# Hybrid encoder block on one core: wide column sums and a new order in the opening, v stores on ScalarE's queue, and two fourth weight sums on GpSimd

## The chip, the cores and the metric

The kernel runs on one core of a Trainium2 chip, in one launch. The time is the device time in microseconds (us) of that core. The engines are TensorE (PE in the profile; its weight loads are shown as PEld), VectorE (DVE), ScalarE (ACT), GpSimd (POOL) and SyncE (SP), which here only issues DMAs. TensorE's products go to PSUM; the other operands lie in SBUF.

## The reference

One encoder layer in float32 on 1024 positions of width 1024, then a final RMSNorm. Cut to what matters here:

```python
ada = silu(c) @ w_ada + b_ada                 # 6 x 1024 values: shift1, scale1, gate1, shift2, scale2, gate2
h = rmsnorm(x, g_mix) * (1 + scale1) + shift1
qa, ka, va, qb, kb, vb, ga, gb = split(h @ w_in)
oa = mixture_of_dilations(qa, ka, va, rel_bias)
ob = neighbourhood_attention_2d(qb, kb, vb, na_rpb)
x = x + gate1 * ((sigmoid(ga) * (oa @ w_branch_dil) + sigmoid(gb) * (ob @ w_branch_na)) @ w_out)
h2 = rmsnorm(x, g_ffn) * (1 + scale2) + shift2
u_val, u_gate = split(conv3(h2 @ w_up))
x = x + gate2 * ((gelu(u_gate) * u_val) @ w_down)
y = rmsnorm(x, g_final)
```

## The kernel before

**Products in three parts.** Nearly every large product is made of three TensorE products of a reduced-precision type: an operand is split into a high half, made by a ScalarE copy, and a low half, the operand less that copy, made by VectorE or GpSimd (`split`, L57 and L61). The three are high x high, high weight x low, low weight x high. So every weight tile passes through ScalarE and VectorE or GpSimd ahead of its product, and so does every tile of h.

**The layout.** x and h are held transposed, as 8 tiles (k = 0 to 7) of 128 features by 512 positions, for two halves of the positions. The program is one function, written out in stages. In the opening (the `with tc.manual_schedule` block, L419 to L610) the order of every engine's instructions is the order of the code. Most of the attention and of the feed-forward part lies outside such blocks: there a scheduler, which simulates a timeline, sets the order, so it can shift far away from an edit.

**The opening.** Needed first is h = x * rstd * (1 + scale1) * g_mix + shift1, the names being `am1` for (1 + scale1) * g_mix and `ada` for the shifts. The first 2048 columns of w_ada are loaded in four pieces (`wt[0]` to `wt[3]`, 8 rows t of 128 x 512 each). Piece q gives shift and scale for the tile pair k = 2q, 2q + 1, so the loop `for q in range(4)` makes h pair by pair. A piece is summed over its 1024 rows in two ways together: `ada_rows` multiplies rows by a column of `cs` (silu of c) and adds them up on VectorE (L174, L176; the running sum `acc` lies in PSUM, the last one goes back into the row's own tile), and `ada_sums` (L160) brings the sum across partitions on TensorE, with each 128 x 128 block of a row as weights and one column, of `cs` or of ones, as the moving operand: four matmuls of one column, a "narrow four". A row that goes straight to `ada_sums` with its column of `cs` is spared VectorE. `piece_bias` (L293, L295) then writes `ada` and `am1`.

At the same time ScalarE squares the tiles of x, VectorE adds the squares, `add_sums` (L98) sums them across partitions, `rs` becomes the reciprocal root (L458, L459, L461), `bcast` (L111) spreads it over the partitions in PSUM (`pb`, with a copy `pbs` in SBUF by ScalarE, L470), and x is multiplied by it: tiles 0 to 3 on VectorE (L473, L481), 4 to 7 on GpSimd (L487). `scaled` makes the high half of h (L229, ScalarE), a full copy (L230, ScalarE) and, when called later, the low half (L231, VectorE). With them run `qk_products` (L310, first q and k tile) and `v_parts` (L320, first v columns).

Between the narrow fours stand `warm(n, ...)` matmuls (L236) of a matrix of ones, 128 columns each, whose result is dropped: they only keep TensorE running.

SyncE's queue issues the loads in the order of the code: x, the small vectors, w_ada piece 0, half of the first weights of q and k (`half_load`), half of v's, piece 1, the other halves, piece 2, piece 3, the second half of x. An issue there also waits for an earlier transfer to land.

**The v products.** `v_out` (L285) copies a v product from PSUM to a buffer `vs` (two of them) on ScalarE and stores it by SyncE's queue (L287). In the loop over `v_steps` these stores alternate in SyncE's queue with loads of later w_ada pieces (`pair_load`, L135), whose rows VectorE sums (`row_pairs`). The loop covers nine of twelve steps; the rest follows it.

**The first w_up tiles.** A w_up tile's product is done by seven products of half size (Strassen's scheme in Winograd's form). `a_operands` makes its weight operands from the quarters a11, a12, a21, a22: S1, S2 and S3 on GpSimd (L1255 to L1257), the fourth sum S4 = a12 - S2 on VectorE (L1273), each followed by a split. It is a generator; each `next` issues one more portion. Tiles t = 0, 1 and 2 are interleaved, with the operands of h2 made in between: each tile of x is multiplied by the broadcast rstd (`scale`, L1622), added or subtracted (L1625, L1631, L1645), and split (L1442, L1443, L1236, L1237).

```python
        pair(ws, ("S2", "S1"), *s_tiles())
        S4 = S1 if apart else a12
        if w_at != 3:
            dve.tensor_tensor(S4, a12, S2, OP.subtract)
        yield
        pair(raw[1], ("S3", "22"), *s_tiles())
```

Of the kernel before, what the change touches and what calls it, by code (L numbers as in the profile page):

```python
# [18 lines left out]
D = 1024  # L19
# [10 lines left out]
def hybrid_encoder(tc, xT, c, w_ada, small, w_in, p1_bias, p23_bias, na_bias, ln2_mult, ident, w_br, w_out,  # L30
# [62 lines left out]
    qkpool = tc.alloc_tile_pool(name="qk", bufs=4)  # L93

# [189 lines left out]
    def v_out(br, st, p, c0=0):  # L284
        vs = work.tile([128, 512], FT, name="vs", bufs=2)[:, :p.shape[-1]]  # L285
        act.activation(vs, p, AF.Copy)
        sp.dma_start((va_s, vb_c)[br][st * 128:st * 128 + 128, c0:c0 + p.shape[-1]], vs)  # L287
# [17 lines left out]
    def qk_products(ks):  # L305
        for k in ks:
            mhi, mlo = h[0, k]
            for x_, (part, m) in enumerate(((0, mhi), (1, mhi), (0, mlo))):
                for p, w in zip(qk_psum, qk_w):
                    pe.matmul(p, w[part][:, k], m, start=k + x_ == 0, stop=k == KT - 1 and x_ == 2)  # L310
# [108 lines left out]
    with tc.manual_schedule(engines={e.engine for e in (sp, act, dve, pool, pe)}):  # L419
# [26 lines left out]
        warm(35, idle, True)  # L446
# [6 lines left out]
        pcol = ps_n.tile([128, KT], FT, name="pcol")  # L453
# [4 lines left out]
        dve.tensor_scalar(r, pcol[:, :4], 1.0 / D, EPS, OP.mult, OP.add)  # L458
        act.activation(r, r, AF.Sqrt)  # L459
        ada_rows(wt[0], acc, range(3, 4), 3, 7)  # L460
# [15 lines left out]
        for q in range(4):  # L476
            ks = range(2 * q, 2 * q + 2)
            piece_bias(q, pa)
            if q == 0:
                for k in range(2, 4):  # L480
                    dve.tensor_tensor(x[0][k], x[0][k], pb, OP.mult)  # L481
                stage = [ps_n.tile([128, 512], FT, name=n) for n in ("pcol", "pbc")]
            low = [scaled(x[0][k], k) for k in ks]
            if q == 0:
                v_split(v_raw, (pool, pool), slice(0, 4), v_w[0])
                for k in range(4, 8):
                    pool.tensor_tensor(x[0][k], x[0][k], pbs, OP.mult)  # L487
# [18 lines left out]
            qk_products(ks)  # L506
            if q == 0:
                pa = ada_sums([(wt[1][t], cs[:, t:t + 1]) for t in (6, 7)], stop=False)
                v_parts(0, range(4), ks, (0,))
                ada_sums([(wt[1][5], ones)], pa)  # L510
                v_parts(0, range(4), ks, (1, 2))
                continue
            v_parts(0, (0,), ks, range(3))
# [26 lines left out]
        row_ends = (4, 7, 10, 12, 14, 17, 19, 22, 24)  # L540
# [37 lines left out]
        for n, step in enumerate(v_steps[:9]):  # L578
# [50 lines left out]
    for br, st in v_steps[9:]:  # L629
        v_out(br, st, *v_wide(st))  # L630
# [612 lines left out]
    def a_operands(raw, n, work, st, lo_eng=pool, last=False, w_at=0, spot=None, apart=False):  # L1243
# [5 lines left out]
        S2, S1 = ws[:, 0], ws[:, 1]  # L1249

# [18 lines left out]
        yield  # L1269
        pair(ws, ("S2", "S1"), *s_tiles())  # L1270
        S4 = S1 if apart else a12
        if w_at != 3:
            dve.tensor_tensor(S4, a12, S2, OP.subtract)  # L1273
        yield
        pair(raw[1], ("S3", "22"), *s_tiles())
# [313 lines left out]
    prep.append(a_operands(raw.pop(1), 4, s_home, sts[1], dve, spot=extra))  # L1589
# [94 lines left out]
    nxt = a_operands(raw.pop(2), 4, s_home, sts[2], w_at=None, spot=extra)  # L1684
# [225 lines left out]
```

## Time and profile before

| | |
|---|---|
| three timed runs, us | 1501.8, 1496.16, 1500.61; median 1500.61 |
| profiled execution, us | 1498.67 |
| its span, first to last instruction, us | 1496.8 |
| mean granted TensorE clock | 0.998 of full speed |
| DMA | 210.29 MB, mean 140 GB/s |

Times in the profile count from the span's start. A row of the timeline gives start, duration, engine, line, operation, the tiles out<-in with shapes, how many instructions it merges, and in brackets the idle time of the engine before it with the instruction that ended it. A float32 matmul leaves two records, so a narrow four shows as x8. Matmuls overlap, and a busy TensorE may still be one that streams fillers.

### The profile page before, as it was taken

What the parts mean: (1) busy time and instruction counts of PE and PEld (TensorE: products, weight loads), DVE (VectorE), ACT (ScalarE), POOL (GpSimd) and SP (SyncE); (2) the same over time, 40 slices, a digit from 0 to 9 for tenths busy, and PEclk for the clock granted to TensorE, in tenths of its full rate; (3) what the DMA queues carried; (4) which work ended last, traced back from release to release, by engine and by line L of the source; (5) the groups of instructions that cost most, each with busy time, mean ns of one, the idle gap of its engine ahead of it and who ended that gap; (6) DMA issues with size and microseconds to landing.
All of it is one profiled execution on the core that took longest, in us unless ns stands there. A gap on an engine that the chain in (4) does not pass through costs nothing.

```text
span 1496.8 us, 21659 instructions
## 1 busy us (share of the span) xinstructions
PE 1474.4 (98%) x7664; PEld 1251.9 (84%) x7664; DVE 939.0 (63%) x1763; ACT 773.6 (52%) x1442; POOL 760.6 (51%) x633
## 2 busy tenths in 40 slices
PE   9999999999999999999999999999999999999997
PEld 8888888889798998888888778888888888877887
DVE  7683446465555665556515897666666667886865
ACT  4531666666655666653345464444444447474542
POOL 3031332434234454512268668766666776978811
PEclk9999999999999999999999999999999999999999
DMA  9577332444645555577544313222222233542313
GB/s 371 183 277 268 88 99 68 143 114 129 170 144 145 144 160 166 172 243 260 194 153 143 104 43 141 85 85 85 85 83 84 71 136 116 197 148 64 104 41 113
DMA packets 117301, 210.29 MB, mean 140 GB/s; under 512 B 42788, under 2 KB 55716, under 8 KB 117156
## 3 DMA queue, kind: packets, MB, share of 16 engines
q1 hardware_dynamic: 116632, 208.57, 43.4%
q8 instruction: 60, 0.98, 0.3%
q14 instruction: 49, 0.40, 0.1%
q10 hardware_dynamic: 560, 0.33, 0.1%
HBM read 163.58 MB, written 42.66 MB: 138 GB/s over the span
## 4 chain that ended last, share of the span: by engine, by line
PE 81%; DVE 5%; POOL 5%; DMA 4%; issue 2%; ACT 2%; SPq 0%; DVEq 0%; POOLq 0%; ACTq 0%
PE pj L84 10%; PE pj L86 10%; PE pj L85 10%; PE pj L1308 10%; PE pj L1307 10%; PE pj L1306 10%; PE pj L402 3%; PE O L1013 2%; DMA wraw<-w_down 2%; PE T L1000 1%; PE S L978 1%; POOL wsl L61 1%; PE pv L279 1%; PE pv L281 1%; PE pv L280 1%
## 5 line engine op out<-in xcount | busy, mean ns | idle before, releaser
L61 POOL TENSOR_TENSOR wlo<-wraw,whi 128x512 fp32r<-128x512 f32 (+1 forms) x84 | 106.1, 1284 | 144.8 <-ACT whi L57 129.8
L84 PE MATMUL pj<-h,whi 128*128 128x512 f32 x432 | 178.1, 412 | 0.4 <-DVE kl L374 0.4
L86 PE MATMUL pj<-h,wlo 128*128 128x512 f32 x432 | 169.8, 393 | 0.0
L85 PE MATMUL pj<-h,whi 128*128 128x512 f32 x432 | 169.4, 392 | 0.0
L1306 PE MATMUL pj<-op,wsh 128*128 128x512 f32 x408 | 159.1, 391 | 3.7 <-ACT wsh L57 2.7
L1307 PE MATMUL pj<-op,wsh 128*128 128x512 f32 x408 | 159.1, 390 | 0.9 <-DVE op L1237 0.6
L1308 PE MATMUL pj<-op,wsl 128*128 128x512 f32 x408 | 157.8, 390 | 0.7 <-POOL wsl L61 0.7
L667 DVE TENSOR_TENSOR tl<-T,th 128x512 fp32r<-128x512 f32 (+3 forms) x120 | 77.2, 654 | 101.2 <-ACT th L666 99.9
L717 POOL TENSOR_TENSOR wlo<-wraw,whi 128x512 fp32r<-128x512 f32 x58 | 74.4, 1293 | 126.8 <-ACT whi L716 126.7
L61 POOL TENSOR_TENSOR wsl<-big,wsh 128x512 fp32r<-128x512 f32 (+1 forms) x86 | 111.7, 1320 | 42.5 <-ACT wsh L57 37.6
L659 ACT ACTIVATE P<-P,st 128x256 f32<-128x256 f32 x128 | 64.2, 503 | 93.9 <-DVE st L658 93.9
L1543 DVE SCALAR_TENSOR_TENSOR big<-pj,sm,big 128x512 f32<-128x512 f32 (+2 forms) x183 | 94.9, 563 | 16.5 <-ACT big L1537 15.6
L86 PEld LDWEIGHTS pj<-h,wlo 128*128 128x128 f32 x432 | 81.1, 188 | 18.0
L1306 PEld LDWEIGHTS pj<-op,wsh 128*128 128x128 f32 x408 | 76.6, 188 | 21.9 <-ACT wsh L57 4.0
L1307 PEld LDWEIGHTS pj<-op,wsh 128*128 128x128 f32 x408 | 76.6, 188 | 18.2 <-DVE op L1237 1.2
L1308 PEld LDWEIGHTS pj<-op,wsl 128*128 128x128 f32 x408 | 76.6, 188 | 17.4 <-POOL wsl L61 1.8
L84 PEld LDWEIGHTS pj<-h,whi 128*128 128x128 f32 x432 | 81.5, 189 | 11.5 <-issue 0.8
L1308 PE MATMUL pj<-op,wlo 128*128 128x512 f32 x232 | 90.3, 389 | 0.0
L1307 PE MATMUL pj<-op,whi 128*128 128x512 f32 x232 | 90.3, 389 | 0.0
L1306 PE MATMUL pj<-op,whi 128*128 128x512 f32 x232 | 90.3, 390 | 0.0
L85 PEld LDWEIGHTS pj<-h,whi 128*128 128x128 f32 x432 | 81.7, 189 | 10.1
L61 POOL TENSOR_TENSOR wsl<-wraw,wsh 128x384 fp32r<-128x384 f32 (+1 forms) x46 | 57.3, 1268 | 62.1 <-ACT wsh L57 54.5
(398 smaller groups left out, 4173.6 us busy)
## 6 DMA issues: line engine op xcount, KB each, us to landing
wraw<-w_in SPq DMA_DIRECT2D x32, 512.0 KB
wada<-w_ada SPq DMA_DIRECT2D x31, 512.0 KB
big<-w_up SPq DMA_DIRECT2D x22, 512.0 KB
wraw<-w_up SPq DMA_DIRECT2D x22, 512.0 KB
big<-as SPq DMA_DIRECT2D x22, 512.0 KB
as<-big SPq DMA_DIRECT2D x21, 512.0 KB
gs<-gs SPq DMA_DIRECT2D x32, 256.0 KB
g<-gs SPq DMA_DIRECT2D x16, 512.0 KB
```

What stands on the lines that cost most here:

```text
L61: lo_eng.tensor_tensor(lo[:, i:i + step], raw[:, i:i + step], f(hi)[:, i:i + step], OP.subtract)
L84: pe.matmul(psum, whi[:, k0 + k], mhi, start=k == 0, stop=False)
L85: pe.matmul(psum, whi[:, k0 + k], mlo, start=False, stop=False)
L86: pe.matmul(psum, wlo[:, k0 + k], mhi, start=False, stop=k == n - 1)
L402: pe.matmul(p[:, 256 * r:256 * r + 256], ww[:, k], m[:, r], start=k + x + r == 0, stop=k == KT - 1 and x == 2, skip_group_check=True)
L659: act.activation(pp, pp, AF.Exp, bias=mi, scale=-1.0, accum_out=li)
L667: dve.tensor_tensor(tl[:m, :n], pt[:m, :n], f(th)[:m, :n], OP.subtract)
L717: pool.tensor_tensor(lo[:, i:i + n], raw[:, i:i + n], f(hi)[:, i:i + n], OP.subtract)
L1306: pe.matmul(psum, whi[:, k], bhi, start=j < 4 and k == 0, stop=False, skip_group_check=True)
L1307: pe.matmul(psum, whi[:, k], blo, start=False, stop=False, skip_group_check=True)
L1308: pe.matmul(psum, wlo[:, k], bhi, start=False, stop=k == n - 1, skip_group_check=True)
L1543: dve.scalar_tensor_tensor(y[:, dst], src, wt, y[:, dst], OP.mult, OP.add)
```

## The change

1. **Wide sums.** `wide_sums` does the sum of a row of blocks with the column spread over 128 columns: four matmuls of 128 columns instead of one, every column of a block holding the same sum; `every` reads the first column of each block. It is used for the square sums and for pieces 0 and 1 of w_ada. The fillers between them go; in front stand 38 instead of 35, before the first product 4 instead of 5.
2. **Opening order.** The first VectorE row of piece 0 stands ahead of the rstd instructions and one more ahead of the reciprocal. The second pair's multiplies move from VectorE to GpSimd. Row 3 of piece 1 goes to TensorE alone. For pieces 2 and 3, two rows instead of two and three stand ahead of the next `piece_bias`.
3. **Load order.** Piece 1 stands ahead of v's first halves, and piece 2 ahead of the second halves of q, k and v.
4. **v stores.** In the loop over `v_steps` the stores go to ScalarE's queue, and the loop has one step more.
5. **Fourth sums.** `a_operands` takes `s4_at`; for tile 1 (3) and tile 2 (2) S4 is a GpSimd instruction at that portion.

```diff
+    def wide_sums(dst, blocks, col, first=False):
+        for m in range(4):
+            cc = slice(m * 128, m * 128 + 128)
+            pe.matmul(dst[:, cc], blocks[:, cc], col.to_broadcast([128, 128]), start=first and m == 0, stop=False,
+                      skip_group_check=True)
+    def every(p):
+        return p.rearrange("p (t c) -> p t c", c=128)[:, :, 0]
...
+        wt.append(ada_load(1))
         half_load(v_raw, (8, 9), 0)
-        wt.append(ada_load(1))
+        wt.append(ada_load(2))
         half_load(qk_raw, (0, 4), 1)
         half_load(v_raw, (8, 9), 1)
-        wt.append(ada_load(2))
         wt.append(ada_rows_load(3))
...
-        warm(35, idle, True)
+        warm(38, idle, True)
...
-        add_sums(pcol, total, True, True)
-        warm(3, idle, True)
-        pa = ada_sums([(wt[0][0], cs[:, 0:1])], stop=False)
+        wide_sums(pcol, total, ones, True)
+        pa = ps_s.tile([128, 512], FT, name="pada", bufs=1)
+        for t in range(2):
+            wide_sums(pa, wt[0][t], cs[:, t:t + 1], t == 0)
         r = wpool.tile([128, KT], FT, name="rs", bufs=2)[:, :4]
-        dve.tensor_scalar(r, pcol[:, :4], 1.0 / D, EPS, OP.mult, OP.add)
+        ada_rows(wt[0], acc, range(3, 4), 3, 7)
+        dve.tensor_scalar(r, every(pcol), 1.0 / D, EPS, OP.mult, OP.add)
         act.activation(r, r, AF.Sqrt)
-        ada_rows(wt[0], acc, range(3, 4), 3, 7)
+        ada_rows(wt[0], acc, range(4, 5), 3, 7)
         dve.reciprocal(r, r)
         qk_split(0, (pool, pool))
         pb = bcast(r, ps_n, "pbc")
-        warm(3, idle, True)
-        ada_sums([(wt[0][1], cs[:, 1:2])], pa, stop=False)
-        warm(4, idle, True)
-        ada_sums([(wt[0][2], cs[:, 2:3])], pa, stop=False)
-        warm(2, idle, True)
+        wide_sums(pa, wt[0][2], cs[:, 2:3])
...
-        ada_rows(wt[0], acc, range(4, 8), 3, 7)
+        ada_rows(wt[0], acc, range(5, 8), 3, 7)
...
-        ada_sums([(wt[0][7], ones)], pa)
-        warm(5, idle, True)
+        wide_sums(pa, wt[0][7], ones)
+        warm(4, idle, True)
...
             if q == 0:
-                for k in range(2, 4):
-                    dve.tensor_tensor(x[0][k], x[0][k], pb, OP.mult)
...
-                for k in range(4, 8):
+                for k in range(2, 8):
                     pool.tensor_tensor(x[0][k], x[0][k], pbs, OP.mult)
...
-            steps = (range(q + 1, 4), range(4, 5), range(5, 7)) if q else (range(0), range(2), range(2, 6))
+            steps = (range(2, 4), range(4, 5), range(5, 7)) if q else ((), (0,), (1, 2, 4, 5))
...
-                ada_rows(wt[q + 2], acc, range(q + 2), 0, 6)
+                ada_rows(wt[q + 2], acc, range(2), 0, 6)
...
+                qk_products((0,), range(2))
+                pa = ps_s.tile([128, 512], FT, name="pada", bufs=1)
+                wide_sums(pa, wt[1][3], cs[:, 3:4], True)
+                qk_products((0,), range(2, 3))
+                qk_products((1,))
...
-                    v_out(step[0], st, pp)
+                    v_out(step[0], st, pp, queue=act)
...
+        if s4_at == 2:
+            pool.tensor_tensor(S4, a12, S2, OP.subtract)
         pair(ws, ("S2", "S1"), *s_tiles())
-        if w_at != 3:
+        if w_at != 3 and not s4_at:
             dve.tensor_tensor(S4, a12, S2, OP.subtract)
         yield
+        if s4_at == 3:
+            pool.tensor_tensor(S4, a12, S2, OP.subtract)
```

TensorE's line in the opening, from the square sums to the first product of h. Before (`pcol` holds the square sums, `pada` those of w_ada, `om` the fillers' ones, `kl` and `qs` the tiles of w_ada piece 0):

```order
L236 MATMUL pv<-om 128x128 x35
L98 MATMUL pcol<-ones,sq 128x1 x4
L236 MATMUL pv<-om 128x128 x3
L160 MATMUL pada<-cs,kl 128x1 x4
L111 MATMUL pbc<-idt,rs 128x128 x4
L236 MATMUL pv<-om 128x128 x4
L160 MATMUL pada<-cs,qs 128x1 x4
L236 MATMUL pv<-om 128x128 x2
L160 MATMUL pada<-ones,qs 128x1 x4
L236 MATMUL pv<-om 128x128 x5
L310 MATMUL pj<-h,whi 128x512 x2
```

And now:

```order
L246 MATMUL pv<-om 128x128 x38
L99 MATMUL pcol<-ones,sq 128x128 x4
L99 MATMUL pada<-cs,kl 128x128 x8
L121 MATMUL pbc<-idt,rs 128x128 x4
L99 MATMUL pada<-cs,qs 128x128 x4
L99 MATMUL pada<-ones,qs 128x128 x4
L246 MATMUL pv<-om 128x128 x4
L321 MATMUL pj<-h,whi 128x512 x2
L321 MATMUL pj<-h,wlo 128x512 x2
L99 MATMUL pada<-cs,wada 128x128 x4
L321 MATMUL pj<-h,whi 128x512 x4
```

The last sum of piece 0 (`pada<-ones,qs`) has no filler ahead of it any more but follows the third row's sum directly, and the sum of piece 1's row 3 has come between the first pair's products.

VectorE's line where the rstd of h2 for the second half of the positions is ready and the tiles of x are multiplied by it. Before (`wraw<-wraw,xb` is S4 of tile 1, `x<-x,pbc` with their numbers the multiplies):

```order
L103 TENSOR_SCALAR rs<-pcol 128x4
L105 RECIPROCAL rs<-rs 128x4
L1273 TENSOR_TENSOR wraw<-wraw,xb 128x512
L1622 TENSOR_TENSOR x_8240<-x_8240,pbc 128x512
L1622 TENSOR_TENSOR x_8277<-x_8277,pbc 128x512
```

GpSimd's line at the same place, now (`xb` and `wraw` hold the sums of tile 1, `wsl` their low halves):

```order
L1269 TENSOR_TENSOR xb<-wraw 128x512
L1270 TENSOR_TENSOR xb<-xb,wraw 128x512
L1271 TENSOR_TENSOR wraw<-wraw 128x512
L1291 TENSOR_TENSOR wraw<-wraw,xb 128x512
L61 TENSOR_TENSOR wsl<-xb,wsh 128x512 x2
L61 TENSOR_TENSOR xb<-wraw,xb 128x512
```

The S4 row has left VectorE's line, where the multiply now follows the reciprocal, and stands on GpSimd ahead of the low halves of S1 and S2. Behind w_up's first tiles the order of w_up and w_down is shifted in places on all engines, which no line of the diff says.

More of the change, by code (lines that the diff above doesn't have):

```diff
@@ L282, in v_wide, with v_out @@
         return ps
-    def v_out(br, st, p, c0=0):
+    def v_out(br, st, p, c0=0, queue=sp):
         vs = work.tile([128, 512], FT, name="vs", bufs=2)[:, :p.shape[-1]]
         act.activation(vs, p, AF.Copy)
-        sp.dma_start((va_s, vb_c)[br][st * 128:st * 128 + 128, c0:c0 + p.shape[-1]], vs)
+        queue.dma_start((va_s, vb_c)[br][st * 128:st * 128 + 128, c0:c0 + p.shape[-1]], vs)
     sig = wpool.tile([128, KT], FT, name="rs", bufs=2)
@@ L303, in qk_split, with qk_products @@
             split(raw[:, 4 * i:4 * i + 4], hi[:, 4 * i:4 * i + 4], lo[:, 4 * i:4 * i + 4], e)
-    def qk_products(ks):
+    def qk_products(ks, parts=range(3)):
         for k in ks:
             mhi, mlo = h[0, k]
-            for x_, (part, m) in enumerate(((0, mhi), (1, mhi), (0, mlo))):
+            for x_ in parts:
+                part, m = ((0, mhi), (1, mhi), (0, mlo))[x_]
                 for p, w in zip(qk_psum, qk_w):
@@ L577, in hybrid_encoder @@
         due = {}
-        for n, step in enumerate(v_steps[:9]):
+        for n, step in enumerate(v_steps[:10]):
             if step is None:
@@ L628, in hybrid_encoder @@
     first_w = w_split(ahead.pop(1), pool)
-    for br, st in v_steps[9:]:
+    for br, st in v_steps[10:]:
         v_out(br, st, *v_wide(st))
@@ L1241, in hybrid_encoder, with a_operands @@
     names = tuple(b for _, b in STEPS)
-    def a_operands(raw, n, work, st, lo_eng=pool, last=False, w_at=0, spot=None, apart=False):
+    def a_operands(raw, n, work, st, lo_eng=pool, last=False, w_at=0, spot=None, apart=False, s4_at=0):
         spot = spot or big
@@ L1249, in a_operands @@
         S2, S1 = ws[:, 0], ws[:, 1]
+        S4 = S1 if apart else a12
         def pair(src, names, hi, lo, eng=pool):
```

18 lines of the change are left out of this document (9 added, 9 removed).

## The prediction

> **What bounds the kernel now.** I read the page first, then busy time by stretches, then the timeline of the places that the change touches. In the page's first part TensorE is the bound:
>
> ```profile
> PE 1474.4 (98%) x7664; PEld 1251.9 (84%) x7664; DVE 939.0 (63%) x1763; ACT 773.6 (52%) x1442; POOL 760.6 (51%) x633
> ```
>
> So only TensorE's own gaps, and work in its first 20 us that is mere filling, can be won. The stretches below (length, then busy time of PE, PEld, DVE, ACT, POOL) hold the places touched, and one stretch of w_down whose order shifts by itself:
>
> ```profile
> core 0: us, PE busy (x) PEld busy (x) DVE busy (x) ACT busy (x) POOL busy (x), PEclk, DMA share, GB/s
> 20.00:53.00 33.00, 31.37 (x206) 26.75 (x206) 26.73 (x41) 20.95 (x34) 15.09 (x12) 1.00 1.00 384
> 120.00:140.00 20.00, 19.27 (x95) 15.64 (x94) 11.15 (x17) 4.67 (x7) 2.53 (x2) 1.00 0.69 255
> 840.00:870.00 30.00, 28.48 (x123) 22.25 (x122) 29.30 (x37) 16.63 (x25) 12.70 (x9) 1.00 0.11 30
> 870.00:890.00 20.00, 18.12 (x79) 14.19 (x78) 20.00 (x33) 10.71 (x15) 14.89 (x11) 1.00 0.19 62
> 1296.00:1400.00 104.00, 100.18 (x433) 80.00 (x432) 80.21 (x118) 65.61 (x114) 84.51 (x83) 1.00 0.34 111
> ```
>
> TensorE's idle time is 1.63 us in the opening after 20 us, 0.73 around 130, 1.52 + 1.88 = 3.40 where w_up begins, 3.82 in 1296 to 1400. VectorE is full from 870 to 890 and nearly so from 840: there it sets the pace. In the opening the DMA engines are full (share 1.00).
>
> **The opening, first pair of tiles.** Rows of the timeline, in order of time (start, duration, engine, line, operation, idle before and who ended it):
>
> ```profile
> 11.30 1.05 PE L98 MATMUL pcol<-ones,sq 128*128 128x1 f32 x8 [0.24 <-DVE sq L452]
> 12.39 0.16 DVE L458 TENSOR_SCALAR rs<-pcol 128x4 f32<-128x4 f32 x1 [1.14 <-PE pcol L98]
> 12.47 0.75 DVE L174 TENSOR_SCALAR pv<-qs,cs 128x512 f32<-128x512 f32 x1
> 13.12 0.17 DVE L461 RECIPROCAL rs<-rs 128x4 f32<-128x4 f32 x1
> 15.63 0.75 DVE L176 SCALAR_TENSOR_TENSOR qs<-qs,cs,pv 128x512 f32<-128x512 f32 x1
> 15.73 1.14 PE L236 MATMUL pv<-om 128*128 128x128 f32 x8
> 16.70 0.95 PE L160 MATMUL pada<-cs,qs 128*128 128x1 f32 x8
> 17.51 0.69 PE L236 MATMUL pv<-om 128*128 128x128 f32 x4
> 18.04 0.95 PE L160 MATMUL pada<-ones,qs 128*128 128x1 f32 x8
> 19.03 0.16 DVE L293 TENSOR_TENSOR ada<-pada,sm 128x4 f32<-128x4 f32 x1 [1.28 <-PE pada L160]
> 19.31 1.28 DVE L481 TENSOR_TENSOR ks<-ks,pbc 128x512 f32<-128x512 f32 x2
> 19.42 0.81 ACT L229 ACTIVATE h<-ks,ada,am 128x512 fp32r<-128x512 f32 x1 [2.99 <-DVE am L295]
> ```
>
> The last row of the sum (L176, 15.63) ends at 16.38, yet its TensorE sum starts at 18.04: four fillers, a narrow sum and two fillers stand in front in TensorE's line. VectorE waits 1.28 us for it, ScalarE 2.99. A wide sum isn't in this trace. The nearest row is the filler, which also streams 128 columns: four of them (eight records) take 16.70 - 15.73 = 0.97; four narrow ones take 17.51 - 16.70 = 0.81, which is the other bound. I take 0.97, the same shape.
>
> The new chain: three more fillers are 6 x 0.121 = 0.73, of which 0.24 was idle, so the square sums start at 11.79. Three wide fours put the broadcast at 14.7. The scale is ready before that: its VectorE part now has one row ahead and one inside (0.75 each); should the row's data come only at 12.47, where it stands now, the reciprocal ends near 14.3, still under cover. The cover is 0.4 us; without it all that follows moves by as much. Broadcast 0.46 and the third wide sum end at 16.1; VectorE's last row ends between 16.2 and 16.6; its wide sum and the two multiplies, side by side, end 17.3 to 17.9. The bias starts about 17.6 instead of 19.03: **1.4 us**. The second pair's two multiplies (L481, 1.28) leave VectorE's line and go to GpSimd.
>
> **The opening, the other pairs.**
>
> ```profile
> 25.43 2.52 POOL L487 TENSOR_TENSOR ks<-ks,mt 128x512 f32<-128x512 f32 x2
> 27.32 0.75 DVE L174 TENSOR_SCALAR pv<-wada,cs 128x512 f32<-128x512 f32 x1 [0.60 <-DMA wada<-w_ada]
> 28.77 0.15 DVE L293 TENSOR_TENSOR ada<-pada,sm 128x4 f32<-128x4 f32 x1
> 28.89 1.12 PE L320 MATMUL pv<-vwl,h 128*128 128x256 f32 x8
> 31.51 0.77 PEld L310 LDWEIGHTS pj<-h,whi 128*128 128x128 f32 x4 [0.64 <-DVE h L231]
> 35.14 1.55 DVE L176 SCALAR_TENSOR_TENSOR pv<-h,cs,pv 128x512 f32<-128x512 f32 x2
> 36.60 0.15 DVE L293 TENSOR_TENSOR ada<-pada,sm 128x4 f32<-128x4 f32 x1
> 38.77 0.74 PE L310 MATMUL pj<-h,whi 128*128 128x512 f32 x2 [0.47 <-ACT h L229]
> 39.43 0.69 DVE L231 TENSOR_TENSOR h<-pcol,h 128x512 fp32r<-128x512 f32 x1 [0.95 <-ACT pcol L230]
> ```
>
> w_ada's third piece is now queued ahead of 1 MB of weight halves: at 384 GB/s 2.7 us earlier, so the 0.60 at 27.32 goes, and the bias of the second pair (28.77) comes before TensorE ends the first pair (30.01). TensorE is then the limit there. It pays the added sum of w_ada's row 3, 0.97, of which I estimate 0.64 in the wait for the low half (the first pair's like that of 31.51): 0.3 lost. It wins the 0.64 at 31.51, since the low half is ready in time, and the 0.47 at 38.77: one of the three rows ahead of L293 (35.14 is two) now comes behind it, into the 0.95 of idle time at 39.43. Sum: 1.4 - 0.3 + 0.64 + 0.47 = 2.2, and 0.1 from the last pairs: **2.3 us**. Lower bound 0.6 (rival a), upper bound 3.0 (the square sums not later, the added sum hidden). After 53 TensorE has no gap until 120, so it is kept.
>
> **The v stores.** Ten stores go from SyncE's to ScalarE's queue.
>
> ```profile
> 94.35 1.17 ACT L286 ACTIVATE vs<-pv 128x512 f32<-128x512 f32 x2 [12.45 <-DMA v<-vs]
> 131.19 0.50 PE L279 MATMUL pv<-vwh,h 128*128 128x512 f32 x1 [0.26 <-ACT vs L286]
> 134.01 1.02 PE L160 MATMUL pada<-ones,sq 128*128 128x1 f32 x8 [0.47 <-DVE ada L167]
> ```
>
> ScalarE waited 12.45 us for a store that stood behind w_ada loads, and those stood behind stores. Apart, neither holds the other; TensorE's 0.26 and 0.47 should go: **0.7 us**. Bounds: 0.73, and nothing if a store on the new queue lands as late. Behind each store wait ScalarE's next split or copy; ScalarE is busy 4.67 of 20 us there, so the issue itself is covered. The Trainium skill (DMA: Bandwidth & Descriptors, "Issuing engines are not separate DMA queues") holds that transfers from all issuing engines share the same 16 engines and interleave; it speaks against a faster store, and by it alone this term would be 0 and the sum 3.6.
>
> **The first w_up tiles.**
>
> ```profile
> 840.01 0.60 PE L111 MATMUL pbc<-idt,rs 128*128 128x128 f32 x4
> 840.27 1.77 DVE L1273 TENSOR_TENSOR wraw<-wraw,xb 128x512 f32<-128x512 f32 x1 [2.03 <-POOL xb L1256]
> 841.45 3.55 POOL L61 TENSOR_TENSOR wsl<-xb,wsh 128x512 fp32r<-128x512 f32 x2
> 841.97 1.27 DVE L1622 TENSOR_TENSOR x<-x,pbc 128x512 f32<-128x512 f32 x2
> 843.88 0.72 ACT L1442 ACTIVATE op<-big,ada 128x512 fp32r<-128x512 f32 x1 [0.68 <-DVE big L1625]
> 845.47 1.78 DVE L1443 SCALAR_TENSOR_TENSOR op<-big,ada,op 128x512 fp32r<-128x512 f32 x1
> 875.52 0.50 PE L1306 MATMUL pj<-x,xb 128*128 128x512 f32 x1 [1.37 <-DVE wc L1316]
> 877.68 0.68 DVE L1273 TENSOR_TENSOR wraw<-wraw,xb 128x512 f32<-128x512 f32 x1
> 881.32 0.50 PE L1307 MATMUL pj<-x,wsh 128*128 128x512 f32 x1 [0.52 <-DVE x L1673]
> ```
>
> The broadcast is done at 840.61, but VectorE stands at the fourth sum until 841.97. Without it the line starts 1.2 earlier. GpSimd now does the sum ahead of its wsl pair, from 841.45, in 1.26 (the duration of one L487): to 842.7; ScalarE's copy of it stands ahead of the operand copy (843.88), which therefore can't come earlier, and L1443 needs that copy: from 844.6 instead of 845.47. So **0.8 us** of lead in a line that has no idle time up to 890 and that ends TensorE's waits. The second sum frees 0.68 at 877.68, of which TensorE can use its last wait, 0.52: **0.5 us**. GpSimd's new operations can hold up VectorE: L1443 took 1.78 beside GpSimd's work, 1.1 more than the fourth sum's 0.68 at 877.68, so each may cost 1.1; bounds 1.3 - 2.2 = -0.9 and +1.3. I take 1.3, since both fall where GpSimd was already working or VectorE reads the broadcast. The Trainium skill (SBUF — State Buffer, "Who interferes with whom") says that VectorE operations with two SBUF inputs and GpSimd's reads exclude each other; the 1.77 of the fourth sum beside GpSimd agrees, and by it the next such operation of VectorE would wait too, an estimated lead of 0.5 instead of 0.8 and a sum of 4.0 instead of 4.3.
>
> **The sum.** 2.3 + 0.7 + 1.3 = 4.3 us. Against the profiled execution's own 1498.67 (span 1496.8 and 1.87 around it) that is 1494.4. It lies 1.94 under the median of the three runs, 1500.61; the mean of all four is 1499.3, less 4.3: **1495.0**.
>
> **The rivals.** (a) GpSimd becomes the opening's bound: the first halves of v's weights now land behind w_ada's second piece, GpSimd's split of them is late, and only then come the second pair's multiplies (1.26 each). For it: that line had no gap at 25.43. Against: the 1 MB ahead is gone too. It decides once the multiplies start past 27.6, for then the first is done only after TensorE's first pair (28.9). Started at 28.0 it is done at 29.3, about when before reads it (28.77 and 0.39 more, as from 19.03 to 19.42), and only 0.47 and 0.1 of the opening are left: 0.6 instead of 2.3, 1496.7. (b) The stores gain nothing, because one is as late on the new queue as on the old: the 0.7 goes, 1495.7. The rule of the Trainium skill on issuing engines, above, would give this. (c) Slower than before: w_down's order, which nobody chose, differs on every engine; between 1296 and 1400 TensorE idles 3.82, with GpSimd busy 84.5 of 104. A queue order with three times these stalls costs 7.6 more: 1502.6. It decides from 4.3 on, an idle time there above 8.1. (d) All upper ends (3.0 + 0.73 + 1.3) and w_down's 3.82 gone: 8.9, 1490.4.
>
> **The numbers.** Forecast 0.55, (a) 0.17, (b) 0.08, (c) 0.10, (d) 0.10. The runs of before spread 3 us to either side, a median of them by about 1.5. Range 1490.5 to 1500.5: it leaves out most of (c) and (d). The bound of 0.5% that a measurement can tell is 7.5 us; faster by that needs (d) or a stretch of luck beside the forecast: 0.14; slower by it only (c)'s far end: 0.04; within: 0.82.
>
> **What would show it.** Right: the first pair's bias at 17.6, TensorE's first product near 18.9; bias of the second pair under 28; no wait of TensorE at 130; the broadcast multiply straight behind the broadcast in w_up; idle time of 840 to 890 near 2. Wrong: ScalarE waiting for v's weights at 22 to 25 with h behind it, wsl waits at 860, or more idle time than 8 between 1296 and 1400.

## The result and the profile after

Seventeen timed runs each give a median of 1495.45 us (1493.26 to 1500.39) after the change against 1499.72 (1496.16 to 1501.91) before: ratio 0.9974, 95% interval 0.9964 to 0.9983, some 4 us faster and inside the 0.5% that was named as no clear change. The profiled execution took 1496.12 (span 1494.3) against 1498.67 (1496.8).

The stretches that the prediction showed of before, in the changed kernel (length, then busy time of PE, PEld, DVE, ACT, POOL, the granted clock, DMA), and one more, 1240 to 1300:

```profile
20.00:53.00 33.00, 32.91 (x235) 29.93 (x234) 26.73 (x40) 20.18 (x32) 18.12 (x14) 1.00 1.03 390
120.00:140.00 20.00, 20.00 (x102) 16.90 (x101) 11.37 (x19) 4.83 (x7) 3.54 (x3) 1.00 0.75 275
840.00:870.00 30.00, 28.50 (x121) 22.12 (x120) 29.58 (x38) 16.42 (x26) 12.42 (x9) 1.00 0.11 36
870.00:890.00 20.00, 18.13 (x76) 13.77 (x75) 19.13 (x34) 11.65 (x15) 16.59 (x13) 1.00 0.16 54
1240.00:1300.00 60.00, 58.27 (x257) 47.92 (x256) 53.86 (x79) 37.56 (x65) 43.62 (x38) 1.00 0.54 187
1296.00:1400.00 104.00, 101.93 (x448) 83.43 (x447) 83.77 (x122) 68.53 (x118) 86.75 (x85) 1.00 0.33 114
```

TensorE's idle time after 20 us in the opening fell from 1.63 to 0.09 us, around 130 from 0.73 to nothing. Where w_up begins it stayed: 1.50 + 1.87 = 3.37 against 3.40. In 1296 to 1400 it fell from 3.82 to 2.07, but in 1240 to 1300 1.73 is new, where before had none:

```profile
1240.00:1300.00 60.00, 60.00 (x267) 49.69 (x266) 55.13 (x83) 39.66 (x67) 45.12 (x41) 1.00 0.50 173
```

Rows of the changed kernel's timeline in the opening:

```profile
16.03 1.16 PE L99 MATMUL pada<-ones,qs 128*128 128x128 f32 x8 [0.19 <-DVE qs L186]
16.16 0.58 ACT L479 ACTIVATE mt<-pbc 128x512 f32<-128x512 f32 x1
16.77 1.28 DVE L482 TENSOR_TENSOR ks<-ks,pbc 128x512 f32<-128x512 f32 x2 [0.80 <-ACT mt L479]
17.97 0.15 DVE L303 TENSOR_TENSOR ada<-pada,sm 128x4 f32<-128x4 f32 x1
19.22 0.73 PE L321 MATMUL pj<-h,whi 128*128 128x512 f32 x2 [1.15 <-ACT h L239]
26.07 5.05 POOL L494 TENSOR_TENSOR ks<-ks,mt 128x512 f32<-128x512 f32 x4
26.83 0.16 DVE L303 TENSOR_TENSOR ada<-pada,sm 128x4 f32<-128x4 f32 x1 [0.24 <-PE pada L99]
```

The last sum starts at 16.03 (before 18.04), the first bias (L303) at 17.97 (before 19.03), the second at 26.83 (before 28.77).

**Leads.** To see where time comes from, each matmul of a trace was paired with the same one of the first trace of before. The lead at a place is the median, over the pairs within 4 us of it, of the start before less the start in the other kernel. Rows count from a span's own start, so what tells is how a lead changes along a row. The columns are places on before's time axis, in us; all kernels but the first are told below.

| kernel | 50 | 150 | 840 | 950 | 1280 | 1320 | 1420 |
|---|---|---|---|---|---|---|---|
| changed kernel | 2.9 | 4.2 | 3.8 | 3.3 | 3.3 | 0.7 | 4.6 |
| opening_alone | 3.1 | 2.9 | 2.9 | 2.8 | 2.8 | 3.5 | 5.1 |
| stores_alone | -0.5 | 0.7 | -0.3 | -0.3 | -0.3 | -0.5 | 3.8 |
| sums_alone | -5.3 | -5.3 | -5.5 | -6.0 | -6.0 | -8.6 | -4.4 |
| no_sums | 2.9 | 4.1 | 4.0 | 4.0 | 4.0 | 4.4 | 6.5 |
| sum1_only | 2.7 | 3.9 | 3.2 | 3.2 | 3.2 | 3.4 | 4.3 |
| free_sums | 2.7 | 3.9 | 3.5 | 4.4 | 4.4 | 1.9 | 6.4 |
| no_sums_copy | 2.9 | 4.0 | 3.8 | 3.8 | 3.8 | 4.1 | 4.6 |
| old_loads | 1.2 | 2.4 | 1.2 | 0.5 | 0.5 | -2.2 | 2.9 |
| muls_vector | 3.0 | 4.2 | 3.5 | 2.8 | 2.8 | 0.1 | 5.1 |
| narrow | -0.6 | 0.7 | 0.2 | -0.3 | -0.3 | -2.8 | 1.5 |
| wide_in_old | -0.2 | -2.0 | -1.9 | -1.9 | -1.9 | -1.2 | 2.9 |
| before_again | -1.3 | -3.3 | -3.2 | -3.3 | -3.3 | -2.9 | -2.0 |

In the changed kernel the opening brings 2.9, the stores 1.2 more, and the first w_up tiles take 0.5 after 840; 0.3 goes just ahead of them, at 837, as it does in no_sums. At 1320 another 2.6 is gone, and by 1420 3.9 comes back. From 1450 to 1470 the granted clock was 0.91 in this execution, which costs the last 1.5 of its lead.

### The profile page after: what moved, and what is told of

It is laid out like the page before. It is cut to its first block, busy times and chain, and to the rows that moved or that the text cites. A ratio compares the mean times of both kernels' runs of the same rounds, so it can differ in the third digit from the quotient of the medians.

```text
span 1494.3 us, 21618 instructions
## 1 busy us (share of the span) xinstructions
PE 1472.5 (99%) x7652; PEld 1252.8 (84%) x7652; DVE 938.1 (63%) x1758; ACT 773.1 (52%) x1442; POOL 766.5 (51%) x637
## 4 chain that ended last, share of the span: by engine, by line
PE 86%; DVE 4%; DMA 3%; POOL 3%; ACT 2%; issue 1%; SPq 0%; DVEq 0%; POOLq 0%; ACTq 0%
PE pj L84 11%; PE pj L86 11%; PE pj L85 11%; PE pj L1323 10%; PE pj L1325 10%; PE pj L1324 10%; PE pj L413 3%; PE O L1026 2%; PE T L1013 1%; PE S L991 1%; PE pv L289 1%; PE pv L291 1%; PE pv L290 1%; PE O L857 1%; PE O L806 1%
```

## The experiments

**One part at a time.** opening_alone takes parts 1 to 3 of the change, stores_alone part 4, sums_alone part 5, and no_sums the changed kernel less part 5. Two of the lines by which they differ from the changed kernel:

```diff
 opening_alone, stores_alone, no_sums:
-    prep.append(a_operands(raw.pop(1), 4, s_home, sts[1], dve, spot=extra, s4_at=3))
+    prep.append(a_operands(raw.pop(1), 4, s_home, sts[1], dve, spot=extra))
...
 opening_alone, sums_alone:
-                    v_out(step[0], st, pp, queue=act)
+                    v_out(step[0], st, pp)
```

> The kernel before with the opening's part alone (wide sums, new order, load order, second pair's multiplies on GpSimd); the v stores and the fourth weight sums stay as they were. My theory, from the landmarks of the changed kernel's trace: the opening carries about 2.9 us of the gain, so the first product after the opening (52.6 us in the kernel before) starts at 49.7, the last wide v product is 2.9 earlier, and the lead reaches w_up's start (834.1 before) as 2.9. End about 2 to 3 us below the kernel before, 1497 on the same scale. Rival: the 2.94 needs the stores too (w_ada's later pieces come sooner because stores leave SyncE's queue), then the first landmark is at 50.5 or later. Second rival: w_up and w_down take back what arrives early, then the landmark at 834 leads by 2.9 and the end by less than 1.5.

> The kernel before with the v stores' part alone (ScalarE's queue for ten stores, with one more step in the row planner's loop); opening and fourth weight sums as they were. My theory: opening landmark 52.6 unmoved, the last wide v product 1.0 to 1.3 us earlier, ScalarE's wait of 12.45 us at 94 shrinks to about 6, and the end comes 0.7 to 1.3 earlier. Rival (the stores gain only because the opening hands over sooner): the last wide v product leads by under 0.5. Rival (the queue change shares the same DMA engines and gains nothing): wait at 94 above 10 us, no lead.

> The kernel before with the two fourth weight sums of w_up's second and third tile on GpSimd, nothing else. My theory: nothing gained; VectorE's first multiply comes about 1.3 us sooner behind the reciprocal, but its row with weights that follows GpSimd's batch of halves starts at the old place (849.6 in the kernel before), since GpSimd's batch is longer by 1.3. Lead at 871 between -0.3 and +0.3, end within 1 us of the kernel before. The prediction's term, as rival: 0.8 us of lead at 871 and 1.3 at 900, end 1.3 earlier. Second rival (longer GpSimd batch makes TensorE wait for low halves): lag of 0.5 to 0.9 at 900.

> The changed kernel with both fourth weight sums back on VectorE. My theory: the same time as the changed kernel within 1 us (1495.5), with landmarks 49.7 and 145.4 and a lead of 4.1 at 834 kept up to 900. Rival (the fourth sums do bring the 1.3 that the prediction gave them and the trace hides it): 1.3 us slower than the changed kernel, lead at 900 only 2.6 to 2.8. Second rival (they cost): lead at 900 above 4.5 and 0.5 to 1 us faster than the changed kernel.

Ratios to the kernel before: opening_alone 0.9983 (0.9973 to 0.9992), stores_alone 0.9993 (0.9979 to 1.0006), sums_alone 1.0010 (0.9998 to 1.0022), no_sums 0.9967 (0.9955 to 0.9979). The opening's lead, 3.1, needs no help from the stores and reaches w_up as 2.9. The stores win their 1.2 without the opening, so that rival falls. In stores_alone 1.1 of it is lost again between 400 and 450, at a wait of 0.92 (418.85) that neither the kernel before nor the changed one has; why isn't shown. What a store costs ScalarE is seen where a copy has to wait until the store of its buffer has landed. Before:

```profile
79.96 0.60 ACT L286 ACTIVATE vs<-pj 128x512 f32<-128x512 f32 x1 [1.37 <-DMA v<-vs]
84.18 1.61 SPq L287 DMA_DIRECT2D v<-vs  x2
```

and in the changed kernel:

```profile
77.02 0.60 ACT L296 ACTIVATE vs<-pj 128x512 f32<-128x512 f32 x1 [1.37 <-DMA v<-vs]
77.65 0.33 ACTq L297 DMA_DIRECT2D v<-vs  x1
84.83 0.60 ACT L296 ACTIVATE vs<-pv 128x512 f32<-128x512 f32 x1 [6.14 <-DMA v<-vs]
```

The wait is 6.14 against 12.45 before (6.04 in stores_alone, 13.11 in opening_alone, which keeps the stores where they were). Before, the store of the copy at 79.96 is issued at 84.18, behind four loads of w_ada, and the next copy into that buffer starts at 94.35: 14.4 us after the first. In the changed kernel the issue follows its copy at once, and the next copy comes after 7.8 us. Of the 6.6 saved, 3.6 lie ahead of the issue and 3.0 between issue and landing. The Trainium skill (DMA: Bandwidth & Descriptors, "Issuing engines are not separate DMA queues") spoke against a gain, since all queues share the engines; the trace shows 6.14 instead of 12.45, so a wait behind other transfers of the same queue was there to be saved. That the 3.0 behind the issue come from loads that now stand behind the store is argued, not shown.

sums_alone went as the second rival to my theory had it, not as the theory: from 840 to 950 it loses 0.5, as the changed kernel does, and no_sums loses nothing. Every kernel with both sums on GpSimd also loses 2.5 to 2.7 from 1280 to 1320, mostly at two waits of TensorE, and no kernel with before's order loses more than 0.2 there. The two in the changed kernel:

```profile
1285.17 0.50 PE L1323 MATMUL pj<-op,big 128*128 128x512 f32 x1 [1.73 <-DVE wc L1333]
1315.52 0.47 PE L1323 MATMUL pj<-op,big 128*128 128x512 f32 x1 [1.45 <-DVE wc L1333]
```

By 1420 nothing of this loss is left. Over 1240 to 1400 TensorE idles 2.64 to 3.80 in the six traces with the changed order and 0.44 to 3.82 in the eight with before's, where its waits come later. From 1280 to 1420 the first gain 1.3 to 2.4 on the first trace of before, the others 0.9 to 4.8. So the loss at 1320 is shown, a loss over w_down is not.

**Which of the two sums.** sum1_only leaves the first (second tile) on GpSimd and puts the second (third tile) back on VectorE. That alone restores before's order of all products in w_up and w_down; with the second sum on GpSimd the scheduler orders them as in the changed kernel. free_sums leaves both sums out, so that its w_up product is another, and keeps the changed kernel's order.

```diff
 sum1_only:
-    nxt = a_operands(raw.pop(2), 4, s_home, sts[2], w_at=None, spot=extra, s4_at=2)
+    nxt = a_operands(raw.pop(2), 4, s_home, sts[2], w_at=None, spot=extra)
 free_sums:
-        if s4_at == 2:
-            pool.tensor_tensor(S4, a12, S2, OP.subtract)
...
-        if s4_at == 3:
-            pool.tensor_tensor(S4, a12, S2, OP.subtract)
```

> The changed kernel with the second of the two fourth sums (third tile) back on VectorE, so that only the second tile's stands on GpSimd; the order in which the products of w_up and w_down follow each other is then that of the kernel before, which the second one alone changes. My theory: the loss of about 2 us between 1240 and 1320 in the changed kernel comes with that order, so it goes (no wait of 1.7 us at 1285), while the 0.3 lost at 836 to 850 and no gain after it stay: lead against the kernel before 4.1 at 834, 3.8 at 870 and 900, and still 3.8 at 1300; timed like the kernel without both sums, some 1.5 us under the changed kernel. Rival (the first sum costs the lead): 3.3 or less at 920. Second rival (the prediction's term): 4.9 at 870.

> The changed kernel with both fourth weight sums left out (the split takes the quarter a12 itself, so the product is another): neither engine does them, and the order of the products is that of the changed kernel. My theory: GpSimd's longer batch, not VectorE's own work, ends VectorE's wait at the operand row behind it (845.7 in the changed kernel), so without the sum on GpSimd that row starts about 1.3 sooner and the lead at 870 rises from 3.8 to 4.6 or more (if the opening's lead at 834 is again 4.1); the 2 us lost between 1240 and 1320 stay, because the order is the same. Rival (neither engine's sum mattered, TensorE is fed just in time by something else): lead at 870 within 0.2 of 3.8. Second rival (the loss at 1240 to 1320 comes from the later operands, not from the order): no wait of 1.7 us at 1285.

sum1_only: 0.9952 (0.9936 to 0.9968). From 840 to 1280 its lead doesn't move: the first sum on GpSimd neither wins nor costs. (At 920 it is 3.2, under the 3.3 that my rival named, but it was 3.2 at 840 already, where I had expected 3.8.) The loss at 1280 to 1320 is gone, as expected; the expected size of the gain, 1.5 us, lies within the intervals. free_sums (0.9961, 0.9947 to 0.9974) gains 0.9 from 840 to 950. With both sums on VectorE (no_sums) this stretch gains nothing, with both on GpSimd it loses 0.5, so they cost 0.9 on VectorE and 1.4 on GpSimd, if the order of the products, which no_sums doesn't share, plays no part. My theory had 0.8 of the gain by 870, a lead of 4.6; only 0.4 came by then (3.9), the rest at 880 to 890, so GpSimd's batch at the first sum explains half of it at most. The loss of 2.5 by 1320 stays: that is the order's, not the operands'.

Why the first sum's 0.8 didn't come is seen in VectorE's line with GpSimd's beside it, in the changed kernel,

```profile
836.81 1.28 DVE L1639 TENSOR_TENSOR x<-x,pbc 128x512 f32<-128x512 f32 x2 [2.42 <-PE pbc L121]
837.59 1.30 POOL L1291 TENSOR_TENSOR wraw<-wraw,xb 128x512 f32<-128x512 f32 x1
838.01 1.43 DVE L1642 TENSOR_TENSOR big<-x,big 128x512 f32<-128x512 f32 x1
841.07 1.78 DVE L1460 SCALAR_TENSOR_TENSOR op<-big,ada,op 128x512 fp32r<-128x512 f32 x1
843.96 1.84 DVE L1460 SCALAR_TENSOR_TENSOR op<-big,ada,op 128x512 fp32r<-128x512 f32 x1
843.97 2.99 POOL L61 TENSOR_TENSOR wlo<-big,whi 128x512 fp32r<-128x512 f32 x2
845.73 1.77 DVE L1642 TENSOR_TENSOR wc<-x,big 128x512 f32<-128x512 f32 x1
847.42 0.68 DVE L1662 TENSOR_TENSOR x<-x,x 128x512 f32<-128x512 f32 x1
```

and in no_sums, with the sum on VectorE (L1286):

```profile
834.08 0.18 DVE L115 RECIPROCAL rs<-rs 128x4 f32<-128x4 f32 x1 [0.27 <-ACT rs L114]
836.30 1.77 DVE L1286 TENSOR_TENSOR wraw<-wraw,xb 128x512 f32<-128x512 f32 x1 [2.04 <-POOL xb L1269]
837.99 1.27 DVE L1635 TENSOR_TENSOR x<-x,pbc 128x512 f32<-128x512 f32 x2
839.19 0.68 DVE L1638 TENSOR_TENSOR big<-x,big 128x512 f32<-128x512 f32 x1
841.50 1.78 DVE L1456 SCALAR_TENSOR_TENSOR op<-big,ada,op 128x512 fp32r<-128x512 f32 x1
844.39 1.29 DVE L1456 SCALAR_TENSOR_TENSOR op<-big,ada,op 128x512 fp32r<-128x512 f32 x1
845.61 1.78 DVE L1638 TENSOR_TENSOR wc<-x,big 128x512 f32<-128x512 f32 x1
847.31 0.68 DVE L1658 TENSOR_TENSOR x<-x,x 128x512 f32<-128x512 f32 x1
```

The multiply starts 1.2 us sooner, as predicted. But an operation of 0.68 to 0.75 takes up to 1.84 where it meets GpSimd at work. Three take 1.77 or more in either kernel: the fourth sum itself, 841.50 and 845.61 with the sum on VectorE; 841.07, 843.96 and 845.73 with it on GpSimd. Two that were shorter have grown by 1.3 together: the addition behind the multiplies (838.01) from 0.68 to 1.43, the operand row at 843.96 from 1.29 to 1.84. So the 1.2 that VectorE starts sooner is spent, and L1662 starts at 847.42 against 847.31. The Trainium skill (SBUF — State Buffer, "Who interferes with whom") says that VectorE operations with two SBUF inputs and GpSimd's reads of SBUF exclude each other. The trace agrees: the rows that grow are of that kind, while the multiplies, whose broadcast lies in PSUM, keep their 0.64 each beside GpSimd. The prediction gave this 0.3 of lead, the trace all of it.

The second sum, in the changed kernel:

```profile
872.11 1.74 POOL L1285 TENSOR_TENSOR wraw<-wraw,xb 128x512 f32<-128x512 f32 x1
872.62 1.78 DVE L1686 TENSOR_TENSOR big<-big,wc 128x512 f32<-128x512 f32 x1
880.80 0.50 PE L1323 MATMUL pj<-op,wsh 128*128 128x512 f32 x1 [0.34 <-ACT wsh L57]
882.18 0.50 PE L1325 MATMUL pj<-op,wsl 128*128 128x512 f32 x1 [0.18 <-POOL wsl L61]
```

It saves VectorE 0.68 and makes L1686 beside it 1.1 longer, and the later split gives TensorE two new waits, 0.34 and 0.18, in place of the 0.52 at 881.32 before. Counted from start to start they lose 0.84 against 0.68; where the rest of the 0.5 goes isn't shown.

**The load order, the multiplies, the copy.** old_loads puts before's order of loads back, muls_vector the second pair's multiplies on VectorE, and no_sums_copy (from no_sums) moves ScalarE's copy of the broadcast ahead of its copies of the q and k weights:

```diff
 old_loads:
-        wt.append(ada_load(1))
         half_load(v_raw, (8, 9), 0)
-        wt.append(ada_load(2))
+        wt.append(ada_load(1))
...
+        wt.append(ada_load(2))
         wt.append(ada_rows_load(3))
 muls_vector:
+                for k in range(2, 4):
+                    dve.tensor_tensor(x[0][k], x[0][k], pb, OP.mult)
...
-                for k in range(2, 8):
+                for k in range(4, 8):
 no_sums_copy:
-        qk_split(0, (pool, pool))
...
         act.activation(pbs, pb, AF.Copy)
+        qk_split(0, (pool, pool))
```

> The changed kernel with the load order of the kernel before (pieces 1 and 2 of w_ada behind the weight halves of v, and of q and k). My theory: the first pair is unchanged (first bias 18.0, a gain of 1.1 against before), but the second pair's bias falls back to 28.2 to 28.8, TensorE then waits, and of the lead of 2.9 at 50 some 1.1 to 1.7 is left. Rival (the order of sums alone carries it, since DMA is full either way): lead at 50 still 2.7 or more. Second rival (the reordered sums without the loads are worse than before): lead below 0.8.

> The changed kernel with the second pair's two multiplies back on VectorE, in the place they had in the kernel before. My theory: VectorE has 1.28 more in its line ahead of the second pair's bias, which then comes at 27.4 to 28.1 instead of 26.8, still under TensorE's end of the first pair (28.5 to 29); so the lead at 50 falls by at most 0.7, to between 2.2 and 2.9. Rival (the move carries the second pair): lead at 50 below 1.9, TensorE waits above 1 near 29. Second rival (GpSimd's multiplies were late in the changed kernel): lead above 3.1.

> The changed kernel without both fourth sums, and with ScalarE's copy of the broadcast (L479) ahead of its two copies of the first q and k weight halves (which wait for their load). My theory: VectorE's multiply at 16.77 waits 0.80 for that copy, since it stands behind copies that wait for DMA; with the copy ahead the multiply starts 0.6 to 0.8 sooner, the first bias at 17.3 to 17.4, the landmark at 52.6 of the kernel before leads by 3.4 to 3.7 instead of 2.93, and the whole is 0.5 to 0.8 faster than without both sums. Rival (the first bias is bound by TensorE's last wide sum of VectorE's rows, 16.03 to 17.2): bias at 17.8 or later, lead 2.9 to 3.1.

old_loads: 0.9985 (0.9976 to 0.9995). First bias 17.82, second 28.60, lead 1.2 at 50: the load order is worth 1.7 of the opening's 2.9, as my theory had it. muls_vector: 0.9962 (0.9949 to 0.9974); second bias at 26.80, lead 3.0. My theory gave it up to 0.7 lost; nothing is, since the bias waits for TensorE's sum either way (0.23 here, 0.24 in the changed kernel). So the move of the multiplies carries nothing. no_sums_copy: 0.9965 (0.9952 to 0.9977), no better than no_sums:

```profile
15.52 0.60 ACT L478 ACTIVATE mt<-pbc 128x512 f32<-128x512 f32 x1 [1.88 <-PE pbc L121]
15.70 0.75 DVE L186 SCALAR_TENSOR_TENSOR qs<-qs,cs,pv 128x512 f32<-128x512 f32 x1
16.36 1.28 DVE L482 TENSOR_TENSOR ks<-ks,pbc 128x512 f32<-128x512 f32 x2
17.70 0.16 DVE L303 TENSOR_TENSOR ada<-pada,sm 128x4 f32<-128x4 f32 x1
```

The wait of 0.80 is gone, but VectorE's last row (L186) ended at 16.45 in this run, so the bias came only 0.27 sooner, and at 50 the lead is again 2.9: my theory falls. The second pair sets the pace from there on: its first tile of h (L239) starts at 27.51 here and at 27.50 in no_sums.

**Width.** narrow is the changed kernel with narrow sums in place of the wide ones, the fillers still gone. wide_in_old is the kernel before with wide sums and all else as it was. before_again is the kernel before once more.

```diff
 narrow:
-            pe.matmul(dst[:, cc], blocks[:, cc], col.to_broadcast([128, 128]), start=first and m == 0, stop=False,
+            pe.matmul(dst[:, m * 128:m * 128 + 1], blocks[:, cc], col, start=first and m == 0, stop=False,
 wide_in_old:
-        add_sums(pcol, total, True, True)
+        wide_sums(pcol, total, ones, True)
...
-        ada_sums([(wt[0][1], cs[:, 1:2])], pa, stop=False)
+        wide_sums(pa, wt[0][1], cs[:, 1:2])
...
-            piece_bias(q, pa)
+            piece_bias(q, pa if q > 1 else every(pa))
```

> The changed kernel with every wide sum as a narrow one (one moving column), the fillers still left out. My theory: a narrow four takes 0.81 where a wide one takes 0.97, so the sums themselves don't end later; first bias at 17.8 to 18.0, lead at 50 within 0.3 of the changed kernel's 2.9, and the granted clock unchanged at 1.00 in 20 to 53: wide sums stand in for fillers and earn no time by being wide. Rival (TensorE's clock needs the streaming): granted clock below 1.00 between 10 and 40 and a lead at 50 below 2.

> The kernel before with wide sums in the place of the narrow ones that the change makes wide, and nothing else: fillers, order of work, loads, stores and fourth sums stay. My theory: the width itself shortens nothing (lead at 50 between -0.5 and 0.1, a wide four being 0.16 longer than a narrow one), but TensorE streams without a break, so that runs with a mean clock of 0.994 or less, 26 of 66 of the kernel before and 9 of 12 of the changed kernel with narrow sums, become rare (at most 2 of 12); median 0 to 1.5 us below the kernel before. Rival (the half clock comes from elsewhere, and the fillers kept it off as well): still 4 or more of 12 at 0.994 or less.

> The kernel before once more, timed against itself and with a second profile. It tells how far one profile of it is repeated. My theory: three kernels with its w_down order gained 0.9 to 4.1 us between 1296 and 1400 on its first profile, by TensorE's idle time there (3.8 in the first profile, 1.2 to 2.2 in theirs), so that place varies from run to run; I expect idle time of 1 to 3.8 there, and a ratio of 1.000 within 0.0012. In the opening TensorE's granted clock is at a half for 10 us or more in about one run of three, by the share of its 66 timed runs with a mean clock up to 0.994 (26). Rival (the place repeats, and what the variants gain there is theirs): idle time of 3.6 to 4.0 between 1296 and 1400.

Stretches of narrow, then of before_again, then of wide_in_old; the granted clock is the third number from the end:

```profile
10.00:20.00 10.00, 9.83 (x70) 9.65 (x69) 6.75 (x14) 4.51 (x8) 2.51 (x2) 0.76 1.02 379
20.00:53.00 33.00, 32.48 (x207) 28.91 (x206) 25.14 (x38) 19.50 (x31) 17.04 (x14) 0.92 1.01 385
```

```profile
20.00:53.00 33.00, 32.32 (x196) 28.70 (x196) 25.53 (x41) 19.78 (x31) 13.77 (x11) 0.90 0.99 383
1296.00:1400.00 104.00, 101.97 (x438) 82.73 (x438) 82.31 (x121) 66.40 (x117) 86.85 (x85) 0.98 0.36 119
```

```profile
20.00:53.00 33.00, 31.24 (x206) 26.63 (x205) 27.10 (x42) 20.97 (x34) 14.88 (x12) 1.00 1.00 384
```

narrow: 0.9997 (0.9983 to 1.0011), 3.5 us less lead at 50. My theory falls, the rival holds: TensorE ran at half its clock from 15.3 to 25.5. before_again (1.0011, 0.9998 to 1.0024) had it too, from 25.9 to 32.8, and so had sums_alone, whose opening is before's, from 14.5 to 28.1. wide_in_old: 0.9987 (0.9976 to 0.9999), without a shorter opening; that is 2 us (0.1 to 3.6), where I had expected 0 to 1.5. None of its 12 runs has a mean clock of 0.994 or less, against 14 of the 29 of the kernel before timed beside them: my theory holds, and here the width is all that differs. The other timed runs say the same. Their mean clock is 0.994 or less in 41 of the 96 runs of the kernel before that went with the experiments (27 of the first 67, not 26 of 66 as my expectations say), and with before's opening (stores_alone, sums_alone, before_again) in 15 of 35; with narrow in 9 of 12; with wide sums (the changed kernel, wide_in_old and the seven others) in 3 of 102. Of the 96, those 41 have a median of 1500.8, the other 55 one of 1498.1: 2.7 us, in four runs of ten. That every one of these runs lost its clock in the opening isn't shown; the three traces at 0.993 or less did.

before_again also tells what the first trace of before is worth: in 1296 to 1400 it idles 2.03 instead of 3.82, with the same order; among the other kernels with that order it is 0.44 to 3.19. The gains of 0.9 to 4.8 from 1280 to 1420 that these show in the table are therefore no gain of theirs, but what this stretch does from run to run. Part of that is the clock: it stands at a half for 3.4 us at 1361 in no_sums_copy and at 1367 in before_again.

## Why the prediction was right, point by point

The total held: 1495.0 was forecast and 1495.45 measured. Its terms held less well.

- **First pair, 1.4: 1.1.** The bias came at 17.97, not 17.6. The multiplies, taken to run beside the wide sum, waited 0.80 for ScalarE's copy, which stood behind two copies that wait for a load. ScalarE's copy was missing from the chain that the prediction added up.
- **Other pairs, 0.9: 1.9.** The bias came ahead of TensorE's end of the first pair, as argued, and the load order carries it (old_loads). The added sum, -0.3, cost nothing: the lead at 28.89 is 1.3. The third pair's 0.47 became 1.1. Rival (a) didn't come: GpSimd's multiplies started at 26.07, not past 27.6, and muls_vector shows that they decide nothing.
- **Stores, 0.7: 1.2.** The right mechanism, mis-sized, and with the third pair by the same error: idle time was taken as what a wait costs. Rows of before:

```profile
37.43 0.88 PE L320 MATMUL pv<-vwl,h 128*128 128x256 f32 x6
130.32 0.39 PE L280 MATMUL pv<-vwl,h 128*128 128x512 f32 x1
130.55 0.39 PE L281 MATMUL pv<-vwh,h 128*128 128x512 f32 x1
133.15 0.39 PE L281 MATMUL pv<-vwh,h 128*128 128x512 f32 x1
```

and of the changed kernel, without the wait:

```profile
35.62 0.88 PE L331 MATMUL pv<-vwl,h 128*128 128x256 f32 x6
36.34 0.63 PE L321 MATMUL pj<-h,whi 128*128 128x512 f32 x2
```

Matmuls start 0.23 apart here (130.32, 130.55). The one at 131.19 starts 0.64 after 130.55: 0.41 lost, where 0.26 shows as idle. The sum at 134.01 starts 0.86 after 133.15: 0.63 lost, 0.47 shown. The product at 38.77 starts 1.34 after 37.43, in the changed kernel 0.72: 0.62 lost, 0.47 shown. Each wait costs 0.15 more than its idle time, which is what one matmul's record overlaps the next (0.39 long, 0.23 apart). The two waits of the stores are 1.04 so counted, of the 1.2. The prediction also had the trace in which they are shortest: they idle 0.73 there, 0.75 to 1.48 in the four other traces without the stores' part, and nothing in the nine with it.
- **Fourth sums, 1.3: -0.5.** The step that failed. That "the line starts 1.2 earlier" came true; that it carries the lead on because it "has no idle time" did not, since its operations beside GpSimd lengthen by what was saved. The nearer price stood in the prediction, 1.1 for an operation that meets GpSimd, with a lower bound of -0.9; it should have been taken.
- **The order of w_up and w_down, rival (c).** Its mechanism is real, the scheduler's reorder by the second sum, with 2.6 lost by 1320 and made up by 1420; its price, 7.6, and its place, 1296 to 1400, were not. In 1296 to 1400 the changed kernel idles less than the first trace of before.
- **What was missing.** The opening of the kernel before runs in part at half clock in some executions (before_again and sums_alone show it; by the mean clocks it may be four of ten); the one profiled execution that the prediction had did not. By the counts and medians above that is an estimated 41/96 x 2.7 = 1.2 us of an average run, which the wide sums take away; wide_in_old, with the wide sums alone, agrees with its 2 us (0.1 to 3.6). So 2.9 + 1.2 - 0.5 from the traces and about 1.2 from the clock, 4.8, stand against the 4.3 measured: that the forecast's total held is luck, since its errors cancelled. What the new order costs over a whole run stays open. With the rest of the change in place, the kernels without the second sum have ratios of 0.9952, 0.9965 and 0.9967, those with it 0.9962 (muls_vector) and 0.9974, and the intervals overlap. sum1_only has the lowest; its median, 1493.42, is 2.0 below the changed kernel's, and the two intervals just overlap. It is the version that I would keep, though that it beats the changed kernel isn't shown.

## What to carry to other kernels

Count what a wait of the bounding engine costs from start to start, against the spacing without it, not from the idle time shown. An operation moved from VectorE to GpSimd is not off VectorE's line where their operations can't overlap: count the operations that will meet, at their lengthened duration. And before trusting one profile, look how the clock of the timed runs spreads: an effect that the profiled execution missed can be a quarter of the gain.

## What the runs showed of the hardware

TensorE's granted clock fell to a half in the opening without TensorE being idle for long: in before_again the largest idle time in any microsecond ahead of it is 0.41, in narrow there is none in the 5 us before. The three openings that did it in a trace have sums of one moving column (before and stores_alone have them too and kept the full clock in their profiled execution); with these spread over 128 columns 3 of 102 runs have a low clock, instead of 41 of 96. The half clock lasted 6.8 us in before_again, 10.2 in narrow, 13.6 in sums_alone and some 3.4 at the end of the changed kernel (1459): steps of 3.4. Single steps of 3.4 stand outside the opening with wide sums as well: near 392 in opening_alone, no_sums, no_sums_copy and muls_vector, and at 136 in wide_in_old, where the step costs 1.6 of lead. So what the width keeps off is the fall in the opening. The Trainium skill (TensorE: Matmul & The Clock Gate, Part 1) has the clock set by an activity window of 3.4 us, with which these lengths agree. Its rule there ("HAM oscillation — how this bites in real kernels") is to have no idle gap above some 3.4 us; that isn't enough here, and the measurement decides.
